# A hybrid attention and RG-LRU block: the first two channel chunks turned over on TensorE, unread products in a wait, the second halves' rests together, and one accumulator last

## The chip, the cores and the metric

The kernel runs on one core of one Trainium2 chip. The metric is device time in microseconds (us) for one execution. Besides the timed runs there is one execution under the hardware profiler. Its page gives the span, which runs from the first to the last instruction of the program and is a little shorter than the device time. All positions in time are counted from the start of that span.

## What is computed

One decoder layer with 1024 tokens and 1024 channels, then a final RMSNorm. Cut to its frame:

```python
mod = c @ w_ada[l] + b_ada[l]
shift, scale, gate = jnp.split(mod, 3, axis=-1)
h = rmsnorm(x, norm_g[l]) * (1.0 + scale[:, None, :]) + shift[:, None, :]
proj = h @ w_in[l]
q, k, v, g_attn, xr, g_rnn, m_attn, m_rnn = jnp.split(proj, SPLIT_POINTS, axis=-1)
...
merged = (jax.nn.sigmoid(m_attn) * (y_attn @ w_attn_proj[l])
          + jax.nn.sigmoid(m_rnn) * (y_rnn @ w_rnn_proj[l]))
x = x + gate[:, None, :] * (merged @ w_out[l])
...
return rmsnorm(x, final_g)
```

Between the two lies windowed attention with sinks for one part of the columns of `proj` and a convolution with a linear recurrence for another. This change concerns only the first lines: how `h` is made, and the first products of `proj`.

## The kernel before

**Numbers in two parts.** Every float32 operand of a large product is kept as a high part, rounded to the type that TensorE reads fast (`float32r`), and a low part, the rest. A product of two such operands is three products of TensorE: high weights by high data, low weights by high data, high weights by low data. `cast` (lines 100 to 104) makes the high part of a weight on ACT and `rest` (106 to 111) its low part on VectorE. `hh` and `hl` hold the high and low parts of `h`.

**Layout.** For the projection `h` is needed with channels on the partitions: eight chunks `kc` of 128 channels by 1024 tokens, each in two halves `hf` of 512 tokens. The host passes `x` both as it is and transposed (`x_t`). The tile `xT[kc]` holds chunk `kc` of the transposed `x`, `xt[i]` holds the rows of tokens 128 i to 128 i + 127.

**The opening** (lines 186 to 528) makes `h` and, while it does so, computes four blocks of 128 columns of `proj`. These are the four entries of `starts`, each with its weights (two halves of 512 rows; the first halves are loaded by `load_wh(i, 0)`, the second by `load_wh(i, 1)`) and its accumulator of two PSUM banks, one for each half of the tokens. Accumulators 0 and 1 are tiles of `psm` ("pmain" in the profile), 2 is `bk[2:]`, and 3 is `bk[:2]`. Together these are 4 x 8 x 2 x 3 = 192 products of 128x128 weights and 128x512 data. The steps:

- `modulate(kc, 0)` and `modulate(kc, 1)` multiply rows of `w_ada` by the broadcast `c_bc` and sum them on VectorE. They give shift and scale of a chunk (`mods`). With the second goes a small instruction that makes `gsc`, (1 + scale) times the gain `norm_g`.
- `square(i)` on ACT or `square_v(i)` on VectorE sums the squares of a row tile into `rr`. `root_of(hf)` takes the root on ACT for four tiles at once.
- `spread(hf)` takes the reciprocal on VectorE and lays it out along the free axis by four transposes of TensorE into `bk[hf]`. ACT copies this to `r_bc`.
- `norm(kc)` multiplies `xT[kc]` by `r_bc` on VectorE (for chunk 0 each half directly by the bank). `high(kc, hf)` and `affine(kc)` apply `gsc` and the shift on ACT, once rounded into `hh` and once in full into `xT[kc]`. `low(kc)` makes `hl` on VectorE. From chunk 2 on, `affine` comes first and `hh` is copied from it (line 491).
- `terms_of` and `mm_k` are the products. "h" means the two with high data, "l" the one with low data.

**Order.** The function runs under a hand-written schedule: PE, ACT, VectorE, GpSimd and SyncE each execute their instructions in the order in which the Python code issues them, and one that waits holds all that are behind it on its engine. All loads of the opening stand in the queue of SyncE (SP). Row tiles and rows of `w_ada` share a ring of seven buffers (`wada`, lines 210 and 225; row tile 6 has a buffer of its own), so that a load may have to wait until what was in the buffer seven loads before has been read for the last time. The loaded weight halves have a ring of six.

Lines 422 to 475 hold the part for chunk 0 and the first halves of the weights, and lines 483 to 526 the loop over chunks 1 to 7, in which chunk `kc` is finished and normalisation and modulation of chunk `kc + 1` are begun. After the opening come the products for v (`v_product`, lines 1459 to 1461), and then the long series of products of line 672.

Of the kernel before, what the change touches and what calls it, by code (L numbers as in the profile page):

```python
# [17 lines left out]
AF = mybir.ActivationFunctionType  # L18
ALU = mybir.AluOpType
# [3 lines left out]
P = 128  # L23
S = 1024
# [9 lines left out]
PK_C, PK_BSH, PK_BSC, PK_NG, PK_CW, PK_CB, PK_BA, PK_BX, PK_LAM = (  # L34
    0, 8, 16, 24, 32, 64, 72, 80, 88)
# [17 lines left out]
def tile_hybrid_block(ctx, tc, x, x_t, pk, rows, posr, posi, c_row, w_ss, w_gate, w_main, w_v,  # L53
# [33 lines left out]
    def pcol(base, i):  # L87
        return pk_t[:, base + i:base + i + 1]
# [73 lines left out]
    def mm_k(ps, w, kc, terms="hl", xh=hh, xl=hl):  # L162
        h, l = w[kc // 4]
        c0 = (kc % 4) * P
        w_h, w_l = h[:, c0:c0 + P], l[:, c0:c0 + P]
        prods = [(w_h, xh), (w_l, xh)] if "h" in terms else []
        if "l" in terms:
            prods.append((w_h, xl))
        for ww, xx in prods:
            for hf in range(2):  # L170
                mm = T.matmul(ps[hf], ww, xx[kc][hf],  # L171
                              start=(kc == 0 and ww is w_h and xx is xh),
                              stop=(kc == KC - 1 and xx is xl))
        return mm
# [11 lines left out]
    starts = []  # L186
    with ExitStack() as st:
# [26 lines left out]
        def load_ss(kc):  # L214
            for a in range(2):
                load_a(kc, a)

        def load_wh(i, h):
            halfw[i, h] = load_half(w_main[i][:, SL[h]])

        def load_xt(kc):
            dma(xT[kc][:], x_t[kc * P:(kc + 1) * P, :])

        def load_x0(i):
            t = xlast if i == 6 else sp.tile([P, D + 1], F32, tag="wada", name="xt", bufs=7)
            dma(t[:, :D], x[i * P:(i + 1) * P, :])
            xt.append(t[:, :D])

        load_a(0, 0)
        for i in range(4):  # L230
            load_x0(i)
        load_xt(0)
        load_a(0, 1)
        load_wh(0, 0)
        load_x0(4)

        make_identity(nc, ident)
# [8 lines left out]
        def modulate(kc, a):  # L246
            jk = sp.tile([P, D + 1], BF16, tag="junk2", name="jk")
            V.scalar_tensor_tensor(out=jk[:], in0=wada[kc, a][:], scalar=1.0, in1=c_bc[:],
                                   op0=ALU.mult, op1=ALU.mult,
                                   accum_out=mods[:, a * 8 + kc:a * 8 + kc + 1])  # L250
            if a:
                V.scalar_tensor_tensor(out=gsc[:, kc:kc + 1], in0=mods[:, 8 + kc:9 + kc],
                                       scalar=1.0, in1=pcol(PK_NG, kc), op0=ALU.add,
                                       op1=ALU.mult)

        def tiny(name, n=64):
            return sp.tile([P, n], F32, name=name)

        def square(i):
            junk = sp.tile([P, D], BF16, tag="junk", name="junk")  # L260
            A.activation(junk[:], xt[i], AF.Square, accum_out=rr[:, i:i + 1])

        def square_v(i):
            jk = sp.tile([P, D + 1], BF16, tag="junk2", name="jk")
            V.scalar_tensor_tensor(out=jk[:, :D], in0=xt[i], scalar=1.0, in1=xt[i],
                                   op0=ALU.mult, op1=ALU.mult, accum_out=rr[:, i:i + 1])
# [95 lines left out]
        def root_of(hf):  # L362
            r1 = rr[:, 4 * hf:4 * hf + 4]
            A.activation(r1, r1, AF.Sqrt, scale=1.0 / D, bias=eps[:])

        def spread(hf):
            r1 = rr[:, 4 * hf:4 * hf + 4]
            V.reciprocal(r1, r1)
            for j in range(4):
                T.transpose(bk[hf][:, j * P:(j + 1) * P], r1[:, j:j + 1].to_broadcast([P, P]),  # L370
                            ident[:])

        def norm(kc, hf=None):
            if hf is not None:
                V.tensor_tensor(out=xT[0][:, SL[hf]], in0=xT[0][:, SL[hf]], in1=bk[hf],
                                op=ALU.mult)
            else:
                V.tensor_tensor(out=xT[kc][:], in0=xT[kc][:], in1=r_bc[:], op=ALU.mult)

        def high(kc, hf):  # L380
            A.activation(hh[kc][hf], xT[kc][:, SL[hf]], AF.Identity,
                         scale=gsc[:, kc:kc + 1], bias=mods[:, kc:kc + 1])

        def affine(kc, sl=slice(0, S)):
            A.activation(xT[kc][:, sl], xT[kc][:, sl], AF.Identity, scale=gsc[:, kc:kc + 1],
                         bias=mods[:, kc:kc + 1])

        def low(kc, hfs=(0, 1)):
            for hf in hfs:
# [22 lines left out]
        def terms_of(kc, hf, accs, terms):  # L412
            for i in accs:
                w, ps = starts[i]
                h_, l_ = w[0]
                cs = slice(kc * P, (kc + 1) * P)
                for ww, xs in ((h_, hh), (l_, hh), (h_, hl)):
                    if (xs is hl) == (terms == "l"):
                        T.matmul(ps[hf], ww[:, cs], xs[kc][hf],
                                 start=(kc == 0 and ww is h_ and xs is hh), stop=False)  # L420
# [1 line left out]
        some(16)  # L422
        square(0)
        modulate(0, 0)
        for i in (5, 6, 7):
            load_x0(i)
        for i in range(1, 4):
            load_wh(i, 0)
        square(1)
        square(2)  # L430
        some(99)
        load_xt(1)
        load_ss(1)
        square(3)
        modulate(0, 1)
        load_xt(2)
        load_ss(2)
        root_of(0)
        spread(0)
        cast_w(0, 0)  # L440
        norm(0, 0)
        high(0, 0)
        rest_w(0, 0)
        terms_of(0, 0, (0,), "h")
        square(4)
        square_v(5)
        affine(0, SL[0])
        low(0, (0,))
        square(6)
        square_v(7)  # L450
        load_xt(3)
        load_ss(3)
        root_of(1)
        spread(1)
        cast_w(1, 0)
        A.copy(r_bc[:, SL[0]], bk[0])
        rest_w(1, 0)
        A.copy(r_bc[:, SL[1]], bk[1])
        norm(0, 1)
        cast_w(2, 0)  # L460
        high(0, 1)
        rest_w(2, 0)
        affine(0, SL[1])
        cast_w(3, 0)
        norm(1)
        modulate(1, 0)
        rest_w(3, 0)
        low(0, (1,))
        modulate(1, 1)
        terms_of(0, 0, (0,), "l")  # L470
        for i in (1, 2, 3):
            for terms in "hl":
                terms_of(0, 0, (i,), terms)
        terms_of(0, 1, range(4), "h")
        terms_of(0, 1, range(4), "l")
        for i in range(2):
            load_wh(i, 1)
# [5 lines left out]
        for kc in range(1, KC):  # L483
            if kc == 1:
                for hf in range(2):
                    high(kc, hf)
                affine(kc)
            else:
                affine(kc)
                for hf in range(2):  # L490
                    A.copy(hh[kc][hf], xT[kc][:, SL[hf]])
            if kc == 2:
                table()
            if kc + 1 < KC:
                norm(kc + 1)
                for a in range(2):
                    modulate(kc + 1, a)
            if kc in (2, 3):
                for i in (0, 1) if kc == 2 else (2, 3):
                    cast_w(i, 1)  # L500
                    rest_w(i, 1)
            low(kc)
            if kc + 4 < KC:
                load_xt(kc + 4)
                load_ss(kc + 4)
            if kc == 3:
                rv = [load_half(w_v[i // 2][:, SL[i % 2]]) for i in range(4)]
            if kc == 1:
                for hf in range(2):
                    terms_of(kc, hf, range(4), "h")  # L510
            elif kc < KC - 1:
                for w, ps in starts:
                    mm_k(ps, w, kc, terms="h")
                for w, ps in starts:
                    mm_k(ps, w, kc - 1, terms="l")
# [1334 lines left out]
```

## Time and profile before

| what | us |
|---|---|
| device time, median of 3 runs | 927.33 |
| lowest and highest of them | 926.05, 927.44 |
| the profiled execution, device time | 926.55 |
| its span | 924.8 |
| VectorE busy in it | 681.3 |
| ACT busy in it | 533.0 |
| end of the opening's last products (line 171, 69.69 + 1.98) | 71.67 |

A row of the timeline gives start, duration, engine, line of the kernel, operation, "out<-in", shape and type, the number of instructions merged into it, and in brackets how long the engine had been idle before and what ended that. SPq and ACTq are the queues' own instructions, which issue DMAs. PE are the products, PEld the loading of their weights. In the groups by line the last numbers are busy time in us and the mean of one in ns, and then the idle time before. Products overlap: the row of one tells its own duration, while the distance of two starts tells what it costs in a stream.

### The profile page before, as it was taken

What the parts mean: (1) busy time and instruction counts of PE and PEld (TensorE: products, weight loads), DVE (VectorE), ACT (ScalarE), POOL (GpSimd) and SP (SyncE); (2) the same over time, 40 slices, a digit from 0 to 9 for tenths busy, and PEclk for the clock granted to TensorE, in tenths of its full rate; (3) what the DMA queues carried; (4) which work ended last, traced back from release to release, by engine and by line L of the source; (5) the groups of instructions that cost most, each with busy time, mean ns of one, the idle gap of its engine ahead of it and who ended that gap; (6) DMA issues with size and microseconds to landing.
All of it is one profiled execution on the core that took longest, in us unless ns stands there. A gap on an engine that the chain in (4) does not pass through costs nothing.

```text
span 924.8 us, 12289 instructions
## 1 busy us (share of the span) xinstructions
PE 900.3 (97%) x4217; PEld 747.5 (81%) x4217; DVE 681.3 (74%) x1042; ACT 533.0 (58%) x1026; POOL 87.6 (9%) x153
## 2 busy tenths in 40 slices
PE   3999999999999999999999999999999999999997
PEld 1789888887888888888887888888888888887886
DVE  6985888888659974986578676899999737657422
ACT  5643655554557755775687785888878622213211
POOL 0110000000000000000000002455354300000000
PEclk9999999999999999999999999999999999999999
DMA  9952547962323450344235258996665197436311
GB/s 350 414 193 94 203 147 265 313 229 105 114 89 116 171 163 31 130 169 157 79 138 193 73 186 294 332 350 221 195 202 167 55 330 237 161 108 234 137 71 66
DMA packets 81700, 168.40 MB, mean 182 GB/s; under 512 B 12755, under 2 KB 29139, under 8 KB 81638
## 3 DMA queue, kind: packets, MB, share of 16 engines
q1 hardware_dynamic: 78596, 159.47, 49.7%
q0 software_dynamic: 2752, 7.83, 2.4%
q8 instruction: 33, 0.54, 0.2%
q10 hardware_dynamic: 290, 0.32, 0.1%
q14 instruction: 29, 0.24, 0.1%
HBM read 118.20 MB, written 49.78 MB: 182 GB/s over the span
## 4 chain that ended last, share of the span: by engine, by line
PE 83%; DVE 7%; DMA 5%; issue 2%; ACT 1%; SPq 0%; POOL 0%; DVEq 0%; ACTq 0%
PE bk L672 44%; PE rp L171 9%; PE pgate L966 5%; PE bk L171 4%; PE rp L1713 4%; PE pmain L1713 4%; PE s_ps L1216 3%; PE pmain L171 3%; PE pv L1288 2%; DMA tt<-tr_d 2%; DMA wo<-w_out 1%; PE pt L1254 1%; DMA wada<-w_ss 1%; PE bk L1461 1%; PE bk L1460 1%
## 5 line engine op out<-in xcount | busy, mean ns | idle before, releaser
L672 PE MATMUL bk<-nh,wl 128*128 128x512 f32 x352 | 137.4, 390 | 0.4 <-DVE wl L108 0.4
L672 PE MATMUL bk<-nh,wh 128*128 128x512 f32 x352 | 137.2, 390 | 0.0
L672 PE MATMUL bk<-nl,wh 128*128 128x512 f32 x352 | 137.1, 390 | 0.0
L108 DVE TENSOR_TENSOR wl<-r,wh 128x512 fp32r<-128x512 f32 x109 | 78.7, 729 | 20.0 <-ACT wh L102 20.0
L102 ACT CAST wh<-r 128x512 fp32r<-128x512 f32 x109 | 66.8, 618 | 44.2 <-PE bk L1461 11.8
L672 PEld LDWEIGHTS bk<-nh,wl 128*128 128x128 f32 x352 | 66.1, 188 | 15.0 <-DVE wl L108 1.4
L672 PEld LDWEIGHTS bk<-nh,wh 128*128 128x128 f32 x352 | 66.1, 188 | 13.6
L672 PEld LDWEIGHTS bk<-nl,wh 128*128 128x128 f32 x352 | 66.1, 188 | 13.6
L672 PE MATMUL bk<-hh,wh 128*128 128x512 f32 x176 | 68.7, 390 | 0.0
L672 PE MATMUL bk<-hh,wl 128*128 128x512 f32 x176 | 68.6, 390 | 0.0
L672 PE MATMUL bk<-hl,wh 128*128 128x512 f32 x176 | 68.6, 390 | 0.0
L108 DVE TENSOR_TENSOR wl<-ws,wh 128x512 fp32r<-128x512 f32 x76 | 51.6, 684 | 0.5 <-ACT wh L102 0.5
L1240 ACT ACTIVATE p<-p,small 128x129 f32<-128x129 f32 x128 | 50.1, 400 | 0.0
L60 POOL DMA_DIRECT2D yh_d<-yh x1 | 0.6, 557 | 493.1 <-ACT yh L1033 493.1
L102 ACT CAST wh<-ws 128x512 fp32r<-128x512 f32 x76 | 45.8, 613 | 1.3 <-DVE ws L694 1.1
L1730 ACT ACTIVATE o<-xo 128x1024 f32<-128x1024 f32 (+2 forms) x10 | 8.9, 889 | 53.2 <-DVE xo L1729 53.2
L672 PEld LDWEIGHTS bk<-hh,wh 128*128 128x128 f32 x176 | 33.1, 188 | 7.6 <-ACT wh L102 0.9
L672 PEld LDWEIGHTS bk<-hl,wh 128*128 128x128 f32 x176 | 33.0, 188 | 6.9
L672 PEld LDWEIGHTS bk<-hh,wl 128*128 128x128 f32 x176 | 33.1, 188 | 6.7
L1216 PE MATMUL s_ps<-ks,qs 128*128 128x256 f32 (+1 forms) x256 | 37.6, 289 | 0.2 <-DVE p L1230 0.2
L672 PE MATMUL bk<-hha,wl 128*128 128x512 f32 x88 | 34.4, 391 | 0.1
L775 ACT ACTIVATE c<-bk 128x512 f32<-128x512 f32 x29 | 17.3, 597 | 29.7 <-PE bk L672 29.6
(381 smaller groups left out, 2277.2 us busy)
## 6 DMA issues: line engine op xcount, KB each, us to landing
r<-w_main SPq DMA_DIRECT2D x100, 256.0 KB, 4.3
wada<-w_ss SPq DMA_DIRECT2D x16, 512.5 KB, 9.1
qs<-q_d SPq DMA_DIRECT2D x16, 512.0 KB, 6.0
ks<-k_d SPq DMA_DIRECT2D x24, 192.0 KB, 4.0
xT<-x_t SPq DMA_DIRECT2D x8, 512.0 KB, 9.0
q_d<-rhi SPq DMA_DIRECT2D x16, 256.0 KB, 4.3
q_d<-rlo SPq DMA_DIRECT2D x16, 256.0 KB, 4.2
sma_d<-c SPq DMA_DIRECT2D x16, 256.0 KB, 2.5
```

Source lines behind the costliest of these rows:

```text
L102: A.copy(dst[0][:], src)
L108: V.tensor_tensor(out=dst[1][:], in0=src, in1=f32(dst[0][:]), op=ALU.subtract)
L171: mm = T.matmul(ps[hf], ww, xx[kc][hf], start=(kc == 0 and ww is w_h and xx is xh), stop=(kc == KC - 1 and xx is xl))
L672: W["pe"] = T.matmul(ps, ww[:, c], b[kc][xx_], start=(first and kc == 0 and i == 0), stop=(kc == 3 and i == 2), skip_group_check=not first)
L775: A.activation(t["t"], s(), AF.Tanh, scale=0.5)
L966: W["pe"] = T.matmul(ps[:, SL[hf]], ww[:, c0:c0 + P], xx_[:, SL[hf]], start=(ic == 0 and i == 0), stop=(ic == 1 and i == 2))
L1216: W["pe"] = T.matmul(o, qs[:, j, qc], ks[:, b, k0 + (0 if n else P):k0 + 256], start=(b == 0), stop=(b == 1))
L1240: A.activation(px[:, j, :], px[:, j, :], AF.Exp, bias=sm[:, 0, j:j + 1], accum_out=sm[:, 1, j:j + 1])
L1254: W["pe"] = T.transpose(pt[:, j, :], px[:, j, 0:P], ident[:])
L1288: W["pe"] = T.matmul(pv[:], b, m[:].rearrange("p j q -> p (j q)"), start=(i == 0), stop=(i == len(prods) - 1))
L1460: T.matmul(o, hh[kc][th][:, ts_], wl[:, cols], start=False, stop=False)
L1713: T.matmul(ps[:, sl], lhs[k][th][:, ts_], w[:, sl], start=(k == 0 and w is h_ and lhs is mh), stop=(k == KC - 1 and lhs is ml))
```

## The change

- Chunks 0 and 1 are no longer loaded transposed and multiplied by `r_bc`. Instead columns 0 to 255 of the row tiles are scaled in place by the reciprocal root (`scale`, six on VectorE, two on ACT) and turned over by TensorE (`turn`) into two free banks, `raw = [bk[1], bk[3]]`. `high` and `affine` of chunk 0 read the bank; chunk 1 is copied from its bank to `xT[1]`.
- `spread` is only for the other chunks' `r_bc` now. For the second half it uses accumulator 1's second bank, and the products of that accumulator come last among those of chunk 0.
- All four first weight halves are loaded ahead of row tile 4 and cast before the first product; all four accumulators begin at once. Behind these eight products stand 14 products into `raw[0]` whose result nothing reads.
- Row tile 7 is loaded after the first half's turning, with the modulation rows of chunk 1 behind it; `square_v` takes tiles 1, 5 and 6, and `square` takes 7.
- `gsc` of chunks 2 to 7 is made on ACT.
- The four second weight halves are cast and their rests taken in chunk 3, after `modulate(4, 1)`, instead of two each in chunks 2 and 3.
- In chunk 2 the low products of chunk 1 come ahead of the high ones of chunk 2.

```diff
         load_a(0, 0)
         for i in range(4):
             load_x0(i)
-        load_xt(0)
         load_a(0, 1)
-        load_wh(0, 0)
+        for i in range(4):
+            load_wh(i, 0)
         load_x0(4)
...
-            if a:
+            if a and kc < 2:
                 V.scalar_tensor_tensor(out=gsc[:, kc:kc + 1], in0=mods[:, 8 + kc:9 + kc],
                                        scalar=1.0, in1=pcol(PK_NG, kc), op0=ALU.add,
                                        op1=ALU.mult)
+            elif a:
+                A.activation(gsc[:, kc:kc + 1], mods[:, 8 + kc:9 + kc], AF.Identity,
+                             scale=pcol(PK_NG, kc), bias=pcol(PK_NG, kc))
...
-        def spread(hf):
+        def invert(hf):
             r1 = rr[:, 4 * hf:4 * hf + 4]
             V.reciprocal(r1, r1)
+
+        def scale(i, eng):
+            o, r1 = xt[i][:, 0:2 * P], rr[:, i:i + 1]
+            if eng is A:
+                A.activation(o, o, AF.Copy, scale=r1)
+            else:
+                V.tensor_scalar(out=o, in0=o, scalar1=r1, scalar2=None, op0=ALU.mult)
+
+        raw = [bk[1], bk[3]]
+
+        def turn(kc, hf):
             for j in range(4):
-                T.transpose(bk[hf][:, j * P:(j + 1) * P], r1[:, j:j + 1].to_broadcast([P, P]),
-                            ident[:])
...
+                T.transpose(raw[kc][:, j * P:(j + 1) * P],
+                            xt[4 * hf + j][:, kc * P:(kc + 1) * P], ident[:])
+
+        def spread(hf, ps):
+            for j in range(4):
+                T.transpose(ps[:, j * P:(j + 1) * P],
+                            rr[:, 4 * hf + j:4 * hf + j + 1].to_broadcast([P, P]), ident[:])
+            A.copy(r_bc[:, SL[hf]], ps)
+
+        def norm(kc):
+            V.tensor_tensor(out=xT[kc][:], in0=xT[kc][:], in1=r_bc[:], op=ALU.mult)
 
         def high(kc, hf):
-            A.activation(hh[kc][hf], xT[kc][:, SL[hf]], AF.Identity,
+            A.activation(hh[kc][hf], xT[kc][:, SL[hf]] if kc else raw[0], AF.Identity,
                          scale=gsc[:, kc:kc + 1], bias=mods[:, kc:kc + 1])
...
         some(16)
         square(0)
         modulate(0, 0)
-        for i in (5, 6, 7):
-            load_x0(i)
-        for i in range(1, 4):
-            load_wh(i, 0)
-        square(1)
+        load_x0(5)
+        load_x0(6)
+        square_v(1)
         square(2)
         some(99)
-        load_xt(1)
-        load_ss(1)
         square(3)
+        root_of(0)
+        invert(0)
+        for i in range(4):
+            scale(i, V)
         modulate(0, 1)
+        for i in range(4):
+            cast_w(i, 0)
+            rest_w(i, 0)
+        turn(0, 0)
+        turn(1, 0)
+        load_x0(7)
+        load_a(1, 0)
+        load_a(1, 1)
         load_xt(2)
         load_ss(2)
-        root_of(0)
-        spread(0)
-        cast_w(0, 0)
-        norm(0, 0)
         high(0, 0)
-        rest_w(0, 0)
-        terms_of(0, 0, (0,), "h")
+        spread(0, bk[0])
+        affine(0, 0)
+        A.copy(xT[1][:, SL[0]], raw[1])
+        terms_of(0, 0, range(4), "h")
+        for _ in range(14):
+            T.matmul(raw[0], starts[0][0][0][0][:, 0:P], hh[0][0], start=True, stop=True)
         square(4)
         square_v(5)
-        affine(0, SL[0])
+        square_v(6)
+        square(7)
+        root_of(1)
         low(0, (0,))
-        square(6)
-        square_v(7)
+        invert(1)
+        for i in range(4, 8):
+            scale(i, V if i < 6 else A)
+        turn(0, 1)
+        turn(1, 1)
         load_xt(3)
         load_ss(3)
-        root_of(1)
-        spread(1)
-        cast_w(1, 0)
-        A.copy(r_bc[:, SL[0]], bk[0])
-        rest_w(1, 0)
-        A.copy(r_bc[:, SL[1]], bk[1])
-        norm(0, 1)
-        cast_w(2, 0)
         high(0, 1)
-        rest_w(2, 0)
-        affine(0, SL[1])
-        cast_w(3, 0)
-        norm(1)
         modulate(1, 0)
-        rest_w(3, 0)
+        A.copy(xT[1][:, SL[1]], raw[1])
+        affine(0, 1)
+        spread(1, starts[1][1][1])
+        modulate(1, 1)
         low(0, (1,))
-        modulate(1, 1)
-        terms_of(0, 0, (0,), "l")
-        for i in (1, 2, 3):
-            for terms in "hl":
-                terms_of(0, 0, (i,), terms)
-        terms_of(0, 1, range(4), "h")
+        terms_of(0, 0, (0, 2, 3), "l")
+        terms_of(0, 1, (0, 2, 3), "h")
+        terms_of(0, 0, (1,), "l")
+        terms_of(0, 1, (1,), "h")
         terms_of(0, 1, range(4), "l")
...
-            if kc in (2, 3):
-                for i in (0, 1) if kc == 2 else (2, 3):
+            if kc == 3:
+                for i in range(4):
                     cast_w(i, 1)
                     rest_w(i, 1)
...
-                for w, ps in starts:
-                    mm_k(ps, w, kc, terms="h")
-                for w, ps in starts:
-                    mm_k(ps, w, kc - 1, terms="l")
+                for k, terms in ((1, "l"), (2, "h")) if kc == 2 else ((kc, "h"), (kc - 1, "l")):
+                    for w, ps in starts:
+                        mm_k(ps, w, k, terms=terms)
```

More of the change, by code (lines that the diff above doesn't have):

```diff
@@ L364, in root_of, with affine @@
             A.activation(r1, r1, AF.Sqrt, scale=1.0 / D, bias=eps[:])
-        def spread(hf):
+        def invert(hf):
             r1 = rr[:, 4 * hf:4 * hf + 4]
             V.reciprocal(r1, r1)
-            for j in range(4):
-                T.transpose(bk[hf][:, j * P:(j + 1) * P], r1[:, j:j + 1].to_broadcast([P, P]),
-                            ident[:])
[L373 to L378, printed above, removed]
+        def scale(i, eng):
[6 more added lines that the diff above has]
+        def turn(kc, hf):
+            for j in range(4):
+                T.transpose(raw[kc][:, j * P:(j + 1) * P],
[7 more added lines that the diff above has]
+            V.tensor_tensor(out=xT[kc][:], in0=xT[kc][:], in1=r_bc[:], op=ALU.mult)
         def high(kc, hf):
-            A.activation(hh[kc][hf], xT[kc][:, SL[hf]], AF.Identity,
+            A.activation(hh[kc][hf], xT[kc][:, SL[hf]] if kc else raw[0], AF.Identity,
                          scale=gsc[:, kc:kc + 1], bias=mods[:, kc:kc + 1])
-        def affine(kc, sl=slice(0, S)):
-            A.activation(xT[kc][:, sl], xT[kc][:, sl], AF.Identity, scale=gsc[:, kc:kc + 1],
-                         bias=mods[:, kc:kc + 1])
+        def affine(kc, hf=None):
+            dst = xT[kc][:] if hf is None else xT[kc][:, SL[hf]]
+            A.activation(dst, dst if hf is None else raw[0], AF.Identity,
+                         scale=gsc[:, kc:kc + 1], bias=mods[:, kc:kc + 1])
         def low(kc, hfs=(0, 1)):
```

## The prediction

> **What bounds the kernel now.** First the page's busy line, then three stretches of the opening in the view by windows (columns: stretch, then busy us and instructions of PE, PEld, DVE, ACT, POOL, clock, DMA share, GB/s).
>
> ```profile
> PE 900.3 (97%) x4217; PEld 747.5 (81%) x4217; DVE 681.3 (74%) x1042; ACT 533.0 (58%) x1026; POOL 87.6 (9%) x153
> ...
> 0.00:16.00 16.00, 4.65 (x8) 1.88 (x8) 8.78 (x38) 8.17 (x14) 0.69 (x6) 1.00 0.87 320
> 16.00:28.00 12.00, 6.54 (x15) 3.48 (x14) 9.34 (x16) 8.16 (x14) 0.00 (x0) 1.00 1.03 417
> 28.00:72.00 44.00, 43.94 (x187) 35.87 (x188) 38.94 (x65) 25.98 (x37) 6.88 (x13) 1.00 0.73 279
> ```
>
> TensorE is the bound: all but full from 28 us on, idle before. What the change can win lies ahead of 28 us, and it reaches the end only if what feeds the opening's 192 products comes earlier too. The timeline tells what ends each wait.
>
> ```profile
> 10.35 0.23 DVE L350 TENSOR_SCALAR trn<-trn 128x128 f32<-128x128 f32 x1
> ...
> 10.82 1.06 ACT L261 ACTIVATE junk<-xt 128x1024 bf16<-128x1024 f32 x1
> ...
> 12.00 0.30 ACT L364 ACTIVATE rr<-rr,eps 128x4 f32<-128x4 f32 x1
> 13.43 1.23 DVE L248 SCALAR_TENSOR_TENSOR jk<-wada,c_bc 128x1025 bf16<-128x1025 f32 x1 [2.85 <-DMA wada<-w_ss]
> 14.28 0.62 ACT L102 CAST wh<-r 128x512 fp32r<-128x512 f32 x1 [1.98 <-DMA r<-w_main]
> ...
> 14.71 0.16 DVE L252 SCALAR_TENSOR_TENSOR gsc<-mods,pk_t 128x1 f32<-128x1 f32 x1
> ...
> 15.10 1.09 PE L370 MATMUL bk<-ident,rr 128*128 128x128 f32 x4 [8.95 <-DVE rr L368]
> ...
> 16.95 0.81 ACT L381 ACTIVATE hha<-xT,mods,gsc 128x512 fp32r<-128x512 f32 x1 [2.06 <-DVE xT L375]
> 17.43 1.22 DVE L265 SCALAR_TENSOR_TENSOR jk<-xt 128x1024 bf16<-128x1024 f32 x1
> ...
> 17.82 0.79 PE L419 MATMUL pmain<-hha,wh 128*128 128x512 f32 x1 [1.63 <-ACT hha L381]
> ...
> 22.04 1.11 PE L370 MATMUL bk<-ident,rr 128*128 128x128 f32 x4 [3.00 <-DVE rr L368]
> 22.18 0.58 ACT L456 COPY r_bc<-bk 128x512 f32<-128x512 f32 x1
> ...
> 22.80 0.78 PE L419 MATMUL pmain<-hla,wh 128*128 128x512 f32 x1
> ...
> 26.77 0.80 PE L419 MATMUL bk<-hha,wh 128*128 128x512 f32 x1 [0.40 <-ACT wh L104]
> ...
> 28.03 0.80 PE L419 MATMUL bk<-hha,wl 128*128 128x512 f32 x1 [0.47 <-DVE wl L110]
> ...
> 30.75 0.63 PE L419 MATMUL bk<-hhb,wh 128*128 128x512 f32 x1
> ...
> 31.18 0.46 PE L419 MATMUL bk<-hhb,wl 128*128 128x512 f32 x1
> ...
> 31.49 0.39 PE L419 MATMUL bk<-hhb,wh 128*128 128x512 f32 x1
> ```
>
> Up to 31.18 us a product takes 0.43 us (30.75 to 31.18), though the clock column says 1.00. From 31.5 us it takes 0.227 (the row of eight below: 1.98 less 0.39, over 7). It switched after 3.2 us without a gap (from 28.03), or 8.4 us after the broken stream began at 22.80.
>
> ```profile
> 29.84 1.22 DVE L378 TENSOR_TENSOR xT<-xT,r_bc 128x1024 f32<-128x1024 f32 x1
> ...
> 32.24 1.23 DVE L248 SCALAR_TENSOR_TENSOR jk<-wada,c_bc 128x1025 bf16<-128x1025 f32 x1
> ...
> 33.51 0.16 DVE L252 SCALAR_TENSOR_TENSOR gsc<-mods,pk_t 128x1 f32<-128x1 f32 x1
> 33.59 0.69 DVE L390 TENSOR_TENSOR hla<-xT,hha 128x512 fp32r<-128x512 f32 x1
> ...
> 37.65 1.12 ACT L102 CAST wh<-r 128x512 fp32r<-128x512 f32 x2
> ...
> 38.54 1.29 DVE L108 TENSOR_TENSOR wl<-r,wh 128x512 fp32r<-128x512 f32 x2
> ...
> 44.63 0.16 DVE L252 SCALAR_TENSOR_TENSOR gsc<-mods,pk_t 128x1 f32<-128x1 f32 x1
> ...
> 44.82 1.25 ACT L385 ACTIVATE xT<-xT,mods,gsc 128x1024 f32<-128x1024 f32 x1 [2.67 <-DVE gsc L252]
> ...
> 46.10 1.15 ACT L491 CAST hh<-xT 128x512 fp32r<-128x512 f32 x2
> ...
> 47.40 0.62 PE L171 MATMUL pmain<-hh,wh 128*128 128x512 f32 x2
> ...
> 52.27 1.14 ACT L491 CAST hh<-xT 128x512 fp32r<-128x512 f32 x2
> ...
> 52.94 1.02 PE L171 MATMUL pmain<-hh,wh 128*128 128x512 f32 x2
> ...
> 69.69 1.98 PE L171 MATMUL pmain<-hl,wh 128*128 128x512 f32 x8
> ```
>
> From `norm(2)` (29.84) VectorE works through a chunk in about 5 us, TensorE in 24 x 0.227 = 5.44. ACT's operand copies for chunk 4 end at 47.25, as the products want them (47.40); those for chunk 5 end at 53.41, when TensorE already waits (the pair at 52.94 takes 1.02). So the opening has two bounds, one behind the other: TensorE's late, slow start, and VectorE's chain from `norm(2)`. A gain must move both.
>
> **The change, part by part.** All times below are estimates from these and the next rows.
>
> ```profile
> GB/s 0 73 244 355 394 416 413 419 413 320 284 419 419 419 411 408 429 420 420 420 417 413 416 407 420 395 421 420 413 407 431 412 417 420 415 412 400 413 420 412
> ...
> L282 DVE TENSOR_SCALAR r<-trn 128x128 f32<-128x128 f32 x1 | 0.2, 227 | 0.0
> ...
> L1730 ACT ACTIVATE o<-xo 128x256 f32<-128x256 f32 x2 | 0.8, 416 | 4.2 <-DVE xo L1729 4.2
> ...
> 577.15 0.60 PE L1254 MATMUL pt<-ident,p 128*128 128x128 f32 x4
> ```
>
> *Loads.* The DMA runs at about 415 GB/s, so 512 KB cost 1.27 us. `load_xt(0)` and `(1)` go: the shift/scale column `a(0,1)`, landing at 13.41, lands at 12.1; the four quarter-megabyte weights follow at 0.63 each, to 14.65, and x4 to x7 at 15.9, 17.2, 18.4, 19.7. `load_x0(7)` reuses x0's buffer and now stands in SP's queue behind TensorE's turning of x0 (about 14.2). Four transfers are then still under way, so I cost it at nothing; without that cover it is late by what it waits past about 15. The same holds for `load_ss(3)` behind the second turning: needed at 32.7, landing about 29.
>
> *First half.* `square_v(1)` puts 1.25 us on VectorE, whose angle steps then end at 11.85 instead of 10.58, still ahead of the root (12.0 to 12.3, set by x3's arrival). Reciprocal 0.17; four scalings of 128x256, not in the trace: between 0.23 (128x128) and 0.69 (128x512) I take 0.30, 0.23 apart, to 13.5. Then `modulate(0,1)` and `gsc(0)` to 14.9, as before (14.87): its load no longer decides. The eight transposes (0.21 apart, by 15.10's row) end by 14.8. ACT's four casts end with the last weight, 14.65 + 0.6 = 15.25, so `high(0,0)` runs 15.25 to 16.06, against 16.95 to 17.76.
>
> *The 22 products.* Eight real and 14 unread ones start at 16.1. Fast they take 22 x 0.227 = 5.0; each us until the switch adds (0.427 - 0.227)/0.427 = 0.47. With a switch 3.2 us after an unbroken start they are issued by 22.6, with 8.4 us by 25.0. If transposes, running from 12.9, count like products, the switch may come at once: 21.1. I take a switch at 21.0 and 23.4, nearer to the unbroken row, since this stream has no gap. The page "TensorE: Matmul & The Clock Gate" of the Trainium skill, "PE-mode transpose", says that transposes don't count as busy; its Part 1 has a free-running window of 3.4 us that must pass busy. By it the switch falls 3.4 to 6.8 us after 16.1, and the products end between 22.7 and 24.2, the kernel between 923.5 and 925.0. No row here settles that.
>
> *Second half.* x7 at 19.7, square 1.06 + 0.2, root 0.3, reciprocal 0.2, then two scalings on each of VectorE and ACT (0.42 each): done by 22.5, hidden behind the unread products. The rests of the weights (4 x 0.6 on VectorE) and two squares (1.22 each) end by 19.7, hidden too. So the turning starts at 23.4 and its first four results stand at 24.0 (0.60, fast). ACT then does `high` 0.8, the copy for channel 1 0.55, `affine` 0.75, and the spread's copy 0.55: 26.65. Hence `norm(2)` at 26.7 instead of 29.84; `norm(0)` and `norm(1)` are gone, and `modulate(1,·)` fits between 22.2 and 24.9. Meanwhile TensorE does its 16 products of chunk 0, accumulator 1 last, from 24.5 to 28.1; only the spread's copy holds that accumulator, and the other nine products come first.
>
> *The loop.* VectorE needs 14.95 from `norm(2)` to `gsc(4)` before (29.84 to 44.79). Two rests (1.2) move behind it and three `gsc` leave (0.08 each): 13.5, so 40.2. On ACT, `gsc` costs 0.2, between nothing and the 0.30 of line 364. Behind that waiting ACT instruction stand the four casts: 2.25 (by 37.65's row), then `affine(4)` 1.25 and the copies 1.15: 45.05 against 47.25. TensorE could start chunk 4 at 43.2 (28.1, 64 products and some 0.5 of waiting for chunk 3's copies), so it waits about 1.6. VectorE is held for the first cast (0.8) and by four rests; chunk 5's operands come at 50.95 against 53.41. At chunks 6 and 7 a cast for v now also stands between `gsc` and `affine` (0.6): chunk 6 loses 0.15, chunk 7 nothing. The swap in chunk 2 (low products of 1 before high of 2) gives ACT 1.8 us more; it hides `affine(2)`.
>
> Sum: 53.41 - 50.95 = 2.5 less 0.15 gives **2.35 us** earlier at the end of the opening, passed on whole, as TensorE is full behind it. The profiled execution took 926.55 (span 924.8), so **924.2**. The three runs' median is 927.33, 0.8 above; I leave this alone, since the clock's switch at 31.3 in the trace is as early as 28.03 allowed, and my 21.0 is not so lucky. A measurement tells about 0.2% from no change: 925.5 and 929.2 around the median.
>
> **The rivals.** *Transposes heat the clock.* Then the turning waits for its scalings, 22.5, and all comes 1.0 earlier: 923.2. For it: TensorE works nearly without a gap from 12.9. Against: four transposes at 22.04 brought no early switch, though gaps followed them. 12%.
>
> *The clock falls back* in the new 1.6 us wait at chunk 4. After 31 us the trace holds no such wait to judge by (chunk 5's is under 0.5), and the one of 1.63 at 17.8 was met slow. Price: 3.2 us of slow products by the unbroken row, or twice that, at 0.47 each: 925.7 to 927.2. By the skill's page (Part 1, "HAM oscillation") only idling beyond about 3.4 us does this. 10%.
>
> *Slow throughout the opening* (the other side): the 12 transposes after the unread products break the count, and the switch comes only from the 16 products that follow. All 22 then end at 25.5, the 12 transposes at 28.05, and the switch falls 3.2 to 8.4 us later. At 31.3 the end is 0.4 later than before: 926.9; at 36.4 chunk 1 ends 2.9 later: **929.5**. It is slower by over 0.2% from a switch at about 35.7. Against it: products broken by gaps of 0.4 sufficed in 8.4 us, and 22 unbroken ones are more. 8%.
>
> **How the numbers follow.** Forecast 60%, its own range 923.3 to 925.7 (switch at 19.3 to 24.5, a tenth of it above 925.5); heating 12%; falling back 10%; slow opening 8%, five of them past 929.2; 10% is for what I haven't seen, three each to faster and slower, four to same. Faster 0.54 + 0.12 + 0.03 = 0.69; same 0.06 + 0.10 + 0.03 + 0.04 = 0.23; slower 0.08. The range 922.8 to 926.6 takes in the first two with half a microsecond of unknown durations, and the better half of the third.
>
> **What would show it.** `high(0,0)` at about 15.3; products 0.227 apart from about 21; the second turning right behind the unread products, not waiting for ACT; `norm(2)` near 26.7; a wait of about 1.6 before chunk 4's products, ended by ACT; the opening's last product near 69.3. I am wrong if the turning finds its scalings unready (x7 late), if chunk 4's wait is missing or above 3, or if products are slow again behind it.

## The result and the profile after

The changed kernel takes 923.7 us (median of 12 runs, 922.1 to 925.7), the kernel before 926.74 in the same comparison (12 runs). The ratio is 0.9963 with a 95% interval of 0.9951 to 0.9976: faster by 3 us. The profiled execution took 924.41 us against 926.55, with a span of 922.7 against 924.8.

The view by windows of the changed kernel, for the stretches shown of before (same columns):

```profile
0.00:16.00 16.00, 6.67 (x16) 3.48 (x16) 12.16 (x46) 9.56 (x17) 0.69 (x6) 1.00 0.87 325
16.00:28.00 12.00, 11.56 (x54) 9.35 (x55) 10.90 (x21) 10.15 (x18) 0.00 (x0) 1.00 1.02 416
28.00:72.00 44.00, 42.98 (x201) 34.78 (x201) 36.69 (x57) 27.24 (x43) 6.45 (x13) 1.00 0.72 277
```

From 16 to 28 us TensorE works 11.56 us with 54 instructions instead of 6.54 with 15. Behind 28 us it is now idle for 1.02 us of the 44, where it was for 0.06. The timeline of the first part:

```profile
12.97 2.07 PE L384 MATMUL bk<-ident,xt 128*128 128x128 f32 x8 [6.89 <-DVE xt L378]
...
15.24 0.76 ACT L397 ACTIVATE hha<-bk,mods,gsc 128x512 fp32r<-128x512 f32 x1
...
16.06 0.67 PE L436 MATMUL pmain<-hha,wh 128*128 128x512 f32 x1 [0.17 <-ACT hha L397]
...
16.57 0.39 PE L436 MATMUL pmain<-hha,wl 128*128 128x512 f32 x1
...
16.80 0.39 PE L436 MATMUL pmain<-hha,wh 128*128 128x512 f32 x1
...
18.19 3.35 PE L469 MATMUL bk<-hha,wh 128*128 128x512 f32 x14
...
21.50 0.62 DVE L378 TENSOR_SCALAR xt<-xt,rr 128x256 f32<-128x256 f32 x2
...
21.91 0.59 PE L384 MATMUL bk<-ident,xt 128*128 128x128 f32 x2 [0.37 <-DVE xt L378]
...
24.65 0.59 ACT L391 COPY r_bc<-pmain 128x512 f32<-128x512 f32 x1
...
25.40 1.22 DVE L394 TENSOR_TENSOR xT<-xT,r_bc 128x1024 f32<-128x1024 f32 x1
```

The second product already comes 0.23 us ahead of the third: from 16.6 us on the products run at the fast distance, not from 21. The unread products end in time, and the second turning waits 0.37 us for its first scaling. `norm(2)` starts at 25.40; before it was 29.84. The loop behind it, by ACT and TensorE:

```profile
38.62 0.39 ACT L256 ACTIVATE gsc<-mods,pk_t 128x1 f32<-128x1 f32 x1 [1.95 <-DVE jk L248]
38.91 1.13 ACT L102 CAST wh<-r 128x512 fp32r<-128x512 f32 x2
39.55 1.29 DVE L108 TENSOR_TENSOR wl<-r,wh 128x512 fp32r<-128x512 f32 x2 [0.97 <-ACT wh L102]
...
42.93 1.02 PE L171 MATMUL pmain<-hh,wh 128*128 128x512 f32 x2 [0.69 <-ACT hh L510]
...
49.22 1.02 PE L171 MATMUL pmain<-hh,wh 128*128 128x512 f32 x2 [0.26 <-ACT hh L510]
```

ACT stands idle for 1.95 us in front of `gsc(4)` and casts the weights only then; VectorE is idle for 0.97 until the first cast is there; TensorE waits for the operands of chunks 4 and 5. The end of the opening is best read from the first product for v, which follows it without a gap:

```profile
67.78 0.28 PE L1477 MATMUL bk<-wh,hha 128*128 128x256 f32 x1
...
623.01 0.73 PE L171 MATMUL rp<-yl,wh 128*128 128x512 f32 x2 [0.50 <-DMA yl<-yl_d]
...
843.22 0.73 PE L1731 MATMUL rp<-wo,hh 128*128 128x512 f32 x2 [1.05 <-ACT wo L1666]
```

Before, that product started at 71.50. So the opening gained 3.72 us, but the span only 2.1. Comparing the start of each later product in the two traces, the lead is 3.72 up to 600 us, 2.97 at the wait at 623 and 2.85 behind it, and 2.21 from a wait for `wo` (843 us) to the end.

### The profile page after: what moved, and what is told of

Its sections match the earlier page's. It is cut to its first block, busy times and chain, and to the rows that moved or that the text cites. A ratio compares the mean times of both kernels' runs of the same rounds, so it can differ in the third digit from the quotient of the medians.

```text
span 922.7 us, 12372 instructions
## 1 busy us (share of the span) xinstructions
PE 903.0 (98%) x4247; PEld 749.7 (81%) x4247; DVE 681.5 (74%) x1041; ACT 536.2 (58%) x1034; POOL 87.4 (9%) x153
## 4 chain that ended last, share of the span: by engine, by line
PE 79%; DMA 10%; DVE 6%; issue 2%; ACT 1%; POOL 0%; SPq 0%; ACTq 0%; DVEq 0%
PE bk L690 44%; PE rp L171 8%; PE pgate L984 5%; PE rp L1731 4%; PE pmain L1731 4%; PE bk L171 3%; PE s_ps L1234 3%; PE pv L1306 2%; PE pmain L171 2%; DMA r<-w_main 2%; DMA wo<-w_out 1%; DMA tt<-tr_d 1%; DMA yl<-yl_d 1%; PE pt L1272 1%; DMA r<-w_rp 1%
```

## The experiments

The questions: what switches TensorE's clock; what sets the end of the opening, TensorE or the chain over VectorE and ACT; what the unread products and the moved casts are worth; and whether the 1.6 us lost late belong to the change. Every kernel left one trace. Four numbers of each trace are collected here in us: the start of `norm(2)`, the start of the first v product, their difference, and what follows up to the end of the span. Behind them stand the median of the runs and its ratio to the kernel before in the same comparison, with the 95% interval.

| kernel | norm(2) | first v product | difference | behind it | median time (runs) | ratio (95%) |
|---|---|---|---|---|---|---|
| before | 29.84 | 71.50 | 41.66 | 853.3 | 926.74 (12) | - |
| before, again | 30.15 | 71.82 | 41.67 | 853.2 | 926.69 (1) | - |
| before, heated | 29.36 | 71.03 | 41.67 | 854.3 | 926.14 (12) | 0.9994 (0.9982 to 1.0005) |
| changed | 25.40 | 67.78 | 42.38 | 854.9 | 923.7 (12) | 0.9963 (0.9951 to 0.9976) |
| changed, again | 25.61 | 67.99 | 42.38 | 854.6 | 923.72 (6) | 0.9960 (0.9945 to 0.9975) |
| no unread products | 25.35 | 67.74 | 42.39 | 853.5 | 923.04 (6) | 0.9959 (0.9943 to 0.9975) |
| chunk 0 turned alone | 27.15 | 69.50 | 42.35 | 853.9 | 925.03 (11) | 0.9986 (0.9977 to 0.9994) |
| casts in two chunks | 26.30 | 69.72 | 43.42 | 855.5 | 925.22 (11) | 0.9981 (0.9972 to 0.9991) |
| gsc on VectorE | 25.42 | 67.08 | 41.66 | 852.8 | 922.96 (5) | 0.9963 (0.9949 to 0.9977) |
| casts ahead of gsc | 25.20 | 66.52 | 41.32 | 855.3 | 922.75 (6) | 0.9950 (0.9935 to 0.9965) |
| ... and low parts on GpSimd | 25.86 | 72.83 | 46.97 | 853.5 | 924.88 (11) | 0.9992 (0.9977 to 1.0007) |
| ... and spread first | 25.09 | 67.00 | 41.91 | 854.1 | 921.88 (6) | 0.9943 (0.9929 to 0.9958) |
| ... and 8 unread products | 24.42 | 66.39 | 41.97 | 852.8 | 922.08 (6) | 0.9946 (0.9933 to 0.9959) |

The medians come from four comparisons, whose medians of before lie between 926.6 and 927.0. The last three are each built on the casts ahead of `gsc`; the last one has the spread first as well. A trace is one execution, and its time need not be the median: it is 3.2 us above for the low parts on GpSimd, 1.7 above for the casts in two chunks, and 1.4 below for `gsc` on VectorE. The twelve runs of the changed kernel alone lie 3.6 us apart. So the columns from the traces, above all the difference, carry the argument on the opening, while the intervals of most neighbouring ratios overlap.

**The changed kernel again.**

> The changed kernel once more. Theory: the 3.7 us that the opening gains are passed on whole up to about 620 us, and given back in part where TensorE then waits for transfers (for yl at 623, for wo at 843 in the first trace, 0.75 us each); as such waits depend on when transfers land, their sum should differ from execution to execution, while the opening gains 3.5 to 3.9 each time. Rival: the two waits are part of the change, as TensorE arrives there earlier than the transfers allow; then they stand in this trace too, within 0.2 us. Median of the runs 922.5 to 925 against 926 to 927.5 before by both.

The ratio to before is 0.9960 (0.9945 to 0.9975). The opening gains 3.5 us, inside what was expected. The list of late waits has 0.3 and 0.8 us for the loads of `yh` and `yl` and none at `wo`, where the first trace has 0.5 for `yl` and 1.0 for `wo`. So the same two waits do not stand there again; but what follows the opening, 854.6 against 854.9, differs by only 0.3 us. This run by itself does not decide between theory and rival.

**The kernel before again** (one run).

> The kernel before once more, for its late waits. Theory (what is lost behind the opening differs from execution to execution): its first v product starts at 71.3 to 72.5 as in the first trace (71.50), but from there to the span's end it takes up to 1.5 us more or less than the 853.3 of that trace. Rival (the losses belong to an earlier opening): within 0.3 us of 853.3.

853.2 against 853.3: the theory's up to 1.5 us of scatter does not show here. But the table's column has kernels with as early an opening at 852.8 (`gsc` on VectorE, 8 unread products) and at 853.5, beside others at 854 to 855.5. So an earlier opening does not always lose late, and equal code behind the opening takes 852.8 to 855.5. The waits for `yh` and `yl` end with their loads, the one for `wo` with ACT's cast of it (line 1666); what makes these late in some traces stays open.

This trace tells something else besides:

```profile
28.68 0.40 PE L419 MATMUL bk<-hla,wh 128*128 128x512 f32 x1
28.92 0.40 PE L419 MATMUL pmain<-hhb,wh 128*128 128x512 f32 x1
...
30.15 1.22 DVE L378 TENSOR_TENSOR xT<-xT,r_bc 128x1024 f32<-128x1024 f32 x1
...
35.97 0.50 PE L171 MATMUL pmain<-hha,wh 128*128 128x512 f32 x1 [0.50 <-ACT hha L491]
```

Its products are 0.23 apart from 28.68 on, while those of the first trace were 0.43 apart up to 31.18. Even so `norm(2)` and the first v product come 0.3 us later than there, at the same distance of 41.67: TensorE now waits for ACT at 35.97. In the kernel before, then, a switch of the clock at least 2.5 us earlier did not bring the end of the opening forward.

**Heating the kernel before.**

```diff
             A.copy(c_bc[:, SL[hf]], bk[2 + hf])
+        for _ in range(50):
+            T.transpose(bk[0][:, 0:P], ident[:], ident[:])
```

> The kernel before with 50 unread transposes of ident on TensorE while it is idle, from about 6.2 us. Theory (transposes count as work for the clock): about 3.3 us after they start their distance goes from 0.213 to 0.108 us, they end by 13.5, and the products at 17.8 are fast if idle stretches of 1.6 to 3 us do not slow the clock again; the opening ends up to 1.5 us earlier, less what VectorE's chain holds back at chunk 5. Rival (transposes don't count, as the skill's page has it): they stay 0.213 apart, end at 16.8, delay the spread by 1.7 us, and the products stay 0.43 apart up to 31 us or longer; slower than before by 0.5 to 1.5 us.

The view by windows of this kernel, for the added transposes alone (columns: stretch, PE busy, PEld busy, clock, DMA share, GB/s), and its timeline:

```profile
6.00:9.00 3.00, 3.00 (x14) 3.00 (x15) 1.00 1.02 415
9.00:11.80 2.80, 2.80 (x15) 2.80 (x14) 1.00 1.02 416
12.00:14.40 2.40, 2.40 (x24) 2.32 (x22) 1.00 0.92 333
...
15.06 0.65 PE L372 MATMUL bk<-ident,rr 128*128 128x128 f32 x4 [0.50 <-DVE rr L370]
17.34 0.50 PE L421 MATMUL pmain<-hha,wh 128*128 128x512 f32 x1 [1.62 <-ACT hha L383]
17.68 0.40 PE L421 MATMUL pmain<-hha,wl 128*128 128x512 f32 x1
...
21.56 1.11 PE L372 MATMUL bk<-ident,rr 128*128 128x128 f32 x4 [3.48 <-DVE rr L370]
```

Up to 11.8 us one transpose takes 0.2 us, from 12 on 0.1. Transposes alone brought the switch, so they count. It came 5.8 us after they began, not 3.3. The four transposes at 15.06 take 0.65, and the clock stayed fast over an idle stretch of 1.62: the products at 17.34 and 17.68 are 0.34 apart, where the kernel before has 0.59 (17.82 and 18.41). It was slow again behind an idle stretch of 3.48: four transposes in 1.11, and products 0.43 apart behind them. So the heat did not last through the opening. The opening gained only 0.47 us, and the time did not measurably change (0.9994, 0.9982 to 1.0005). `norm(2)` moved by 0.48, and the difference stayed 41.67.

**No unread products.**

```diff
-        for _ in range(14):
-            T.matmul(raw[0], starts[0][0][0][0][:, 0:P], hh[0][0], start=True, stop=True)
```

> The changed kernel without the 14 unread products. TensorE is idle from about 18.2 to 21.9 us. Theory: the clock falls back in that wait, the second turning and some 3.3 us behind it run slow (products 0.43 apart until about 25.3), and the opening ends 0.5 to 1.5 us later than with them: part of the delay is hidden, since ACT and VectorE set the times at chunks 3 to 5. Rival: a wait of 3.7 us isn't enough to slow the clock; products behind it are 0.227 apart and the time is that of the changed kernel.

The windows of this kernel for TensorE alone (stretch, busy, clock, DMA share, GB/s), and its timeline:

```profile
18.00:21.90 3.90, 0.12 (x1) 1.00 1.02 417
21.90:26.40 4.50, 4.49 (x18) 0.62 1.02 414
...
21.91 0.55 PE L384 MATMUL bk<-ident,xt 128*128 128x128 f32 x2 [3.79 <-ACT rr L367]
...
23.18 1.06 PE L389 MATMUL pmain<-ident,rr 128*128 128x128 f32 x4
```

The clock did fall back, with a granted 0.62, as the theory has it: the first transposes at 21.91 are still fast, the four at 23.18 slow. But the opening ends at the same place (67.74) and the time is not worse (0.9959 against 0.9960 of the changed kernel in the same comparison). What the starts of TensorE's products behind 30 us lie further apart than 0.227, at the waits for chunks 3 to 5, sums up to 0.8 us instead of 2.5: it lost its time ahead of waits that it had anyway. The 14 unread products are worth nothing that can be measured here. Both halves of the expectation's theory hold on TensorE; its price at the end, 0.5 to 1.5, does not.

**Only chunk 0 turned over.**

```diff
-        turn(1, 0)
         load_x0(7)
+        load_xt(1)
...
-        A.copy(xT[1][:, SL[0]], raw[1])
...
-        turn(1, 1)
...
-        A.copy(xT[1][:, SL[1]], raw[1])
...
         low(0, (1,))
+        norm(1)
```

> The changed kernel with only chunk 0 turned over by TensorE; chunk 1 is loaded transposed (512 KB, behind row tile 7) and multiplied by r_bc on VectorE, as before. Theory (VectorE's chain from norm(2) sets the opening's end): norm(1) puts 1.14 us ahead of norm(2), which starts at about 26.5 instead of 25.4, and the opening ends 1.0 to 1.3 us later. Rival (TensorE's start and clock set it): norm(2) is later, the opening's end stays within 0.3 us.

`norm(2)` starts 1.75 us later and the first v product 1.72 later: the difference, 42.35, is that of the changed kernel. 1.13 us of it is `norm(1)`. The rest, 0.62, stands ahead of `norm(1)`, which starts at 26.02. It goes with the clock: here it switched late, at 20.6, and the unread products held the second turning until 23.29. The end moved with `norm(2)`, as the theory has it. But TensorE came later here as well, so it is the kernel before again and the one without unread products that speak against the rival.

**The casts in chunks 2 and 3.**

```diff
-            if kc == 3:
-                for i in range(4):
+            if kc in (2, 3):
+                for i in (0, 1) if kc == 2 else (2, 3):
                     cast_w(i, 1)
                     rest_w(i, 1)
```

> The changed kernel with two casts and rests of the second weight halves in chunk 2 and two in chunk 3, as before the change, but gsc still on ACT. Theory (it is the place behind ACT's waiting gsc that costs, not that the four stand together): VectorE is then held twice for its first cast, about 0.9 us each, so chunk 5's operands come 0.5 to 1 us later than in the changed kernel, the wait at chunk 4 moves partly to chunk 3, and the opening ends 0.5 to 1 us later (68.3 to 69.0). Rival (that they stand together is what costs): the wait at chunk 4 shrinks and the opening ends up to 1 us earlier.

The timeline of VectorE, with what ended its idle time:

```profile
35.66 1.30 DVE L108 TENSOR_TENSOR wl<-r,wh 128x512 fp32r<-128x512 f32 x2 [0.97 <-ACT wh L102]
42.69 1.29 DVE L110 SCALAR_TENSOR_TENSOR wl<-r,wh 128x512 fp32r<-128x512 f32 x2 [0.98 <-ACT wh L104]
```

VectorE is held twice instead of once, and the difference grows by 1.04 us to 43.42. The end, 69.72, lies beyond the expected 68.3 to 69.0, as `norm(2)` came 0.9 later too, at 26.30. The edit stands behind `norm(2)` and cannot have moved it; in this trace the clock switched at 19.8 and the unread products held the second turning until 23.09.

**gsc on VectorE, and the casts ahead of gsc.** The first puts `if a:` in place of `if a and kc < 2:`. The second is:

```diff
+            if kc == 3:
+                for i in range(4):
+                    cast_w(i, 1)
             if kc + 1 < KC:
                 norm(kc + 1)
                 for a in range(2):
                     modulate(kc + 1, a)
             if kc == 3:
                 for i in range(4):
-                    cast_w(i, 1)
                     rest_w(i, 1)
```

> The changed kernel with gsc of all chunks on VectorE, as before the change. Theory: ACT then runs the four casts right behind the copies of chunk 3 (from about 36.7), VectorE isn't held for them (0.97), affine(4) starts at about 39; each gsc costs VectorE 0.08 to 0.12 and starts affine 0.2 sooner. The opening ends 0.8 to 1.3 us earlier than in the changed kernel (66.5 to 67.1), as with the casts ahead. Rival (gsc on ACT is a saving, as VectorE's chain is the bound): the opening ends 0.1 to 0.5 us later.

> The changed kernel with ACT's four casts of the second weight halves ahead of the gsc of chunk 4 instead of behind it (the rests stay where they are). Theory: behind the waiting gsc the casts cost TensorE's wait at chunk 4 (1.3 us) and hold VectorE for 0.97; ahead of it, both go: chunk 4's products start without a wait, norm(5) is 0.9 to 1.0 earlier, and TensorE's waits up to chunk 5 sum up to about 1 us less, so the opening ends 0.9 to 1.0 us earlier. Rival: VectorE's chain sets chunk 5 anyway, and the wait moves there whole: no gain.

The difference falls by 0.72 to 41.66 with `gsc` on VectorE, and by 1.06 to 41.32 with the casts ahead. In both ACT casts in its idle time and VectorE is not held. In the second the wait at chunk 4 is gone, and that at chunk 5 grows from 0.26 to 0.48:

```profile
36.38 1.14 ACT L102 CAST wh<-r 128x512 fp32r<-128x512 f32 x2
...
38.30 1.29 DVE L108 TENSOR_TENSOR wl<-r,wh 128x512 fp32r<-128x512 f32 x2
...
47.96 1.02 PE L171 MATMUL pmain<-hh,wh 128*128 128x512 f32 x2 [0.48 <-ACT hh L510]
```

Both theories hold for the opening: it ends 1.26 us earlier with the casts ahead (0.9 to 1.0 expected) and 0.70 with `gsc` on VectorE, just short of the expected 0.8 to 1.3. In the time of whole runs neither is clear of the changed kernel: 0.9950 and 0.9963 against 0.9960 and 0.9963, with intervals that overlap.

**Low parts on GpSimd.**

```diff
-                V.tensor_tensor(out=hl[kc][hf], in0=xT[kc][:, SL[hf]], in1=f32(hh[kc][hf]),
-                                op=ALU.subtract)
+                (G if kc in (3, 4, 5) else V).tensor_tensor(
+                    out=hl[kc][hf], in0=xT[kc][:, SL[hf]], in1=f32(hh[kc][hf]),
+                    op=ALU.subtract)
```

> The kernel with the casts ahead (opening's end 66.5 in its trace), and besides the low parts of chunks 3, 4 and 5 made on GpSimd instead of VectorE (1.3 us for 128x512 there by the row of line 1761's subtraction-like product, 0.69 on VectorE). Theory (VectorE's chain is the bound): norm(5) and norm(6) are 1.2 and 2.4 us earlier, TensorE's wait at chunk 5 (1.1 us) goes, only some 0.5 at chunk 3 stays; the opening ends at 65.3 to 65.8. Rival: GpSimd waits for its own transfers of the angle table until about 41 us and takes 2.6 us a chunk, so the low products wait, or VectorE is slowed while GpSimd works; no gain or a loss.

The rival's second half came true in the trace, and far beyond its size:

```profile
41.37 6.50 DVE L394 TENSOR_TENSOR xT<-xT,r_bc 128x1024 f32<-128x1024 f32 x1
41.76 1.30 POOL L407 TENSOR_TENSOR hla<-xT,hha 128x512 fp32r<-128x512 f32 x1
43.01 1.29 POOL L407 TENSOR_TENSOR hlb<-xT,hhb 128x512 fp32r<-128x512 f32 x1
44.26 2.53 POOL L407 TENSOR_TENSOR hl<-xT,hh 128x512 fp32r<-128x512 f32 x2
...
52.69 1.31 PE L171 MATMUL pmain<-hh,wh 128*128 128x512 f32 x2 [4.55 <-ACT hh L511]
52.71 4.49 POOL L407 TENSOR_TENSOR hl<-xT,hh 128x512 fp32r<-128x512 f32 x2 [5.93 <-ACT hh L511]
...
53.76 2.30 DVE L394 TENSOR_TENSOR xT<-xT,r_bc 128x1024 f32<-128x1024 f32 x1
...
55.98 2.32 DVE L248 SCALAR_TENSOR_TENSOR jk<-wada,c_bc 128x1025 bf16<-128x1025 f32 x1
```

VectorE's multiplication, 1.22 us elsewhere, takes 6.50: it ends 1.1 us after the last of the four GpSimd instructions, which keep their own 1.3 us each. The operands of chunk 5 come late by this, TensorE waits 4.55 us for them, and the opening ended 5 us later than in the changed kernel. At the low parts of chunk 5 the two engines meet again, and there both are slowed: GpSimd's instructions take 2.3 us each, and so do VectorE's. The time of this execution, 928.05, is 3.2 us above the median; seven of the eleven runs lie at 924.3 to 925.4, and no trace shows one of them. So how often VectorE is held for so long is open. There is no gain: the median, 924.88, is 2.1 us above that of the casts ahead.

**Spread first, and fewer unread products.** On top of the casts ahead:

```diff
         modulate(1, 0)
-        A.copy(xT[1][:, SL[1]], raw[1])
-        affine(0, 1)
         spread(1, starts[1][1][1])
+        A.copy(xT[1][:, SL[1]], raw[1])
+        affine(0, 1)
         modulate(1, 1)
+        norm(2)
         low(0, (1,))
...
-                norm(kc + 1)
+                if kc > 1:
+                    norm(kc + 1)
```

> The kernel with the casts ahead, and besides the second spread's transposes and copy ahead of chunk 1's copy and affine(0, 1), and norm(2) ahead of low(0, 1) on VectorE. Theory (the opening ends a fixed 41.3 us behind the start of norm(2) in this order of the loop): norm(2) starts at about 24.65 instead of 25.2 to 25.4 where the turning is early, the first v product at 65.9 to 66.3; where the clock switches late and the unread products hold the turning, all up to 1 us later. Median 0.3 to 0.8 us below the casts-ahead kernel. Rival: chunk 0's products are now held by affine(0, 1) and TensorE becomes the bound; no gain.

> The same with 8 unread products instead of 14. Theory: in executions whose clock switches late (product distance 0.43 up to 19 or 20.6 us) 14 unread products end at 21.6 to 23.1 and hold the second turning, which is ready at 21.9; eight end by 20.9 at the latest, so the second turning always starts when its first scaling is done (21.8 to 22.0), and the idle stretch of 1 to 2 us does not slow the clock (1.6 us did not in the heated kernel before, 3.5 and 3.8 did). Same opening in an early switch, up to 1 us earlier in a late one, so the median is 0 to 0.5 us below the version with 14. Rival: the clock falls back, products behind the turning are 0.43 apart; the opening ends up to 1 us later.

Both beat the kernel before: 0.9943 of it (0.9929 to 0.9958) and 0.9946 (0.9933 to 0.9959), that is 4.5 to 4.7 us faster. Their medians are also 1.6 to 1.8 us below that of the changed kernel, but it was measured in another comparison, and the intervals of the ratios overlap a little. Between the two the runs don't tell. The theory's constant of 41.3 did not hold: `low(0, 1)` now stands behind `norm(2)`, and the difference is 41.9, so of the 0.78 us by which `norm(2)` is earlier in the last trace some 0.6 are paid back. The rival is there in part: the products of chunk 0 are held for some 0.5 us, but TensorE does not become the bound. In the trace with 14 the second turning started at 22.35, as row tile 7 came late there (its square starts at 20.22, with 8 at 19.55); with 8 at 21.69, the clock having switched at 18.7, and it stayed fast over the idle stretch of 0.62.

## Why the prediction came out

The forecast was 924.2, the median is 923.7. By its own steps:

- **First half.** `high(0, 0)` was put at 15.25 and came at 15.24; the angle steps, the scalings and the casts lie where they were put.
- **The clock's switch** was the mis-sized term: 21.0 assumed, with 16.1 if transposes count. The products behind the first turning became fast at 16.1 to 16.9 in three traces, at about 17 to 20.6 in the other seven; in all but two of these ten openings that is earlier than 3.2 us behind the first product (about 19.3). The first rival, with 12%, is what happened in the first trace. The Trainium skill, "TensorE: Matmul & The Clock Gate", "PE-mode transpose", has it that transposes don't count as busy in the same way; the heated kernel shows that they do count here (from 0.2 to 0.1 us within a row of transposes).
- **`norm(2)`** came at 25.40 where 26.7 was forecast. The forecast let it wait for the second turning behind the unread products and for ACT's four steps behind that. In the trace the products were through first, and the turning waited 0.37 us for its scaling: the prediction named this as a sign that it is wrong. Row tile 7, which it suspected for that case, was not late (its square starts at 19.77, 19.7 put); the products were early. From the scaling at 21.50 VectorE then works without a gap up to `norm(2)`, and ACT's copy to `r_bc` is done at 25.24, just ahead of it. That the unread products decide the second turning holds where the switch is late: they reach up to it in four traces, at 21.84, 22.64, 23.09 and 23.29 us.
- **The loop.** Forecast from `norm(2)` to the end of the opening's last product: 42.6 (26.7 to 69.3). Measured from `norm(2)` to the first v product: 42.38; in the kernel before that product starts 0.17 ahead of the other's end, so the two are equal to 0.1 us. `gsc` on ACT took 0.39 instead of 0.2. The wait before chunk 4 is there, ended by ACT as forecast, with 1.3 us by the distances of the starts where 1.6 was put. That the loop's new order costs time was right: 0.72 us of the 4.44 that `norm(2)` gained go there (42.38 less 41.66), and both experiments that free ACT's casts give it back.
- **Passed on whole** was wrong in the trace: 1.6 us of 3.72 were lost in waits for `yl` and `wo` behind 620 us. The openings of the two traces of the changed kernel are 3.5 to 3.7 us earlier, and its medians 3.0 and 3.3. How much of this is chance is open, see above. The two errors, a clock too late by some 1.3 us at `norm(2)` and nothing lost late, had opposite signs: the opening gained 3.72 us where 2.35 was forecast, and late waits took part of it back. That the total came within 0.5 us of the forecast is in part luck.
- **The other rivals.** The clock did not fall back at chunk 4 (the products from 43.79 on are 0.23 apart), and no opening was slow throughout.

## What to carry to other kernels

Look for the one instruction from which the rest of a stage takes a fixed time: here the end of the opening lay 42.4 us behind the start of `norm(2)` in four traces of three kernels whose TensorE did quite different things, and each edit could be priced by whether it moves that start or that distance. An instruction that waits for another engine should stand behind what its own engine could do meanwhile: a tiny one ahead of four casts cost up to 1.06 us. Filling TensorE's idle time to keep its clock brought nothing here, since TensorE lost the time that it gained in later waits.

## What the runs showed of the hardware

- The switch of TensorE's clock differs from execution to execution of the same code. In nine openings whose instructions up to there are the same, and which start TensorE at 12.7 to 13.4 us, it came at 16.1 to 19.8; in the two traces of the kernel before, at 31.2 us and by 28.7.
- The granted clock reads 1.00 while products are still 0.43 apart at the start, and 0.62 once the clock has fallen back behind an idle stretch of 3.79 us. Slow products at the start have to be read from their distance.
- In one trace a VectorE instruction with two operands in SBUF took 5.3 us longer while GpSimd ran four subtractions in a row. The Trainium skill, "SBUF — State Buffer", "Who interferes with whom", says that such a VectorE instruction contends with a GpSimd instruction that reads SBUF, and that issue order decides who blocks. The trace agrees on the contention. It does not show the engine that issues first going first: VectorE's instruction was issued first (41.37 against 41.76) and still ended only 1.1 us behind the last of the four. Some 10 us later in the same trace both engines were slowed instead, to 2.3 us for an instruction (1.3 and 1.2 elsewhere).
